# Weight combinations of a seven-product scheme: from sums on VectorE and GpSimd to accumulating DMA transfers

## The chip, the cores and the metric

One core of a Trainium2 chip runs the kernel. The metric is the device time of one execution in microseconds (us); of several runs the median counts, and lower is better.

## What is computed

The reference is one inference step of a decoder layer for 520 tokens (512 of a prompt and 8 single samples): an RMS norm, an input projection, two groups of heads, an output projection, and then a feed-forward part. The change concerns the feed-forward part alone:

```
h = rms_norm(x, g_ffn_pre)
f = (silu(h @ w_gate) * (h @ w_up)) @ w_down
x = x + rms_norm(f, g_ffn_post)
```

h has 2048 features, w_gate and w_up are 2048 x 5632, w_down is 5632 x 2048, all in fp32.

## The kernel before, in words

**Layout.** Activations lie with features on the 128 partitions and 520 tokens in the free dimension, in two halves of 260 tokens (`cols(0)`, `cols(1)`). A product of fp32 values is made of three matmuls on rounded halves: `halved` (L80 to L85) takes a raw weight tile of 128 x 1024 and writes `wh`, a copy rounded by ScalarE (L82), and `wl`, the rest, by VectorE (L84). `split` does the same for activations. Each of the two tags `wh` and `wl` has 4 buffers, so the weights of a product can be prepared at most four products ahead of TensorE.

**The stage of the seven products.** Four of the 44 row blocks of w_gate and w_up are computed plainly. The other 40 go two at a time, so there are 20 passes of the loop over i, each with one call of `seven` for w_gate and one for w_up: 40 calls, here called groups. In a group a 2 x 2 block of weight tiles (rows i and i+1, input halves 0 and 1: w11, w12, w21, w22) meets a 2 x 2 block of activations (feature halves by token halves). Seven products take the place of eight. Each is a call of `term` (L731): 8 blocks of 128 features by 3 matmuls, 24 matmuls of 128 x 260. The activation combinations T1 to T4 are made once, by `combine` (L656), while the last plain blocks run.

**The weights of a group.** `quarters` (L700) gives seven functions, one for each product, which `pieces` calls in order, two products ahead of the one being computed. They load the four raw tiles by SP's DMA queue (L707) and make the combinations: VectorE forms w21 + w22 (L717) and from it s2 = w21 + w22 - w11 (L719); GpSimd forms w11 - w21 (L720) and w12 - s2 (L725). Raw tiles lie in two pools of tag `wr`: `wx` with 4 buffers and `wp` with 3; the sums lie in buffers of `wh` and `wl`. The results in PSUM are joined by VectorE and ScalarE (L750 to L776), and each pass stores its two row blocks to DRAM (fd, L795).

**What sets the order.** A scheduler writes one order of instructions for each engine and each DMA queue when the kernel is built. At run time every engine and queue takes its instructions strictly in that order, and each waits for the semaphores of what it needs. A DMA issued by SP goes by SP's queue, one issued by GpSimd by GpSimd's.

## Time and profile before

| what | value |
| --- | --- |
| median of 3 runs | 2328.52 us (2328.05 to 2331.99) |
| the profiled execution's own time | 2318.88 us |
| its span in the profile | 2317.2 us |
| TensorE (PE) busy | 2266.3 us, 98% of the span |
| VectorE (DVE) busy | 1664.3 us, 72% |
| ScalarE (ACT) busy | 1065.9 us, 46% |
| GpSimd (POOL) busy | 220.6 us, 10% |
| DMA | 310.16 MB, mean 134 GB/s |

The profile is that of one execution; times in it count from the start of its span. PE is the matmul unit, PEld its weight loads. The slices of the page divide the span into 40 equal parts, with one digit of busy tenths for each; PEclk is the granted clock of TensorE. A matmul's end in the profile is modelled, so busy PE is a share of time with matmuls under way, and its count in a stretch tells how many were done.

### The profile page before, as it was taken

The numbers are of one execution on the slowest core, as the hardware profiler recorded it, in microseconds if no ns is written. First come the engines' busy times: TensorE is split into PE (matmuls) and PEld (weight loads), VectorE is DVE, ScalarE is ACT, GpSimd is POOL, SyncE is SP. The second block draws the span as 40 slices with busy tenths as digits, with TensorE's granted clock in tenths as the row PEclk, the third lists the DMA queues.
The fourth block names the chain that finished last, engine by engine and source line by source line (L and its number), as shares of the span: only waits on it lengthen the run. The fifth ranks groups of instructions, "written<-read, shape, count | busy, mean of one in ns | idle before, by whom it ended". The sixth has DMA issues, their size and how long they took to land.

```text
span 2317.2 us, 44793 instructions
## 1 busy us (share of the span) xinstructions
PE 2266.3 (98%) x18548; PEld 2256.2 (97%) x18548; DVE 1664.3 (72%) x2688; ACT 1065.9 (46%) x1607; POOL 220.6 (10%) x116
## 2 busy tenths in 40 slices
PE   8999999999999998999999999999999999999998
PEld 8999999999999998999999999999999999999998
DVE  8398777777555778888888888888888534434367
ACT  7286566666345555444343443444334512212155
POOL 0000000000000000322222222222221000000000
PEclk9999999999999999999999999999999999999999
DMA  6224333443335766543333333333333723332275
GB/s 224 92 88 125 113 114 111 120 120 120 115 110 182 214 209 194 176 158 115 115 110 126 119 115 124 119 120 110 118 119 102 229 92 129 112 113 95 90 240 156
DMA packets 130267, 310.16 MB, mean 134 GB/s; under 512 B 14928, under 2 KB 57360, under 8 KB 130064
## 3 DMA queue, kind: packets, MB, share of 16 engines
q1 hardware_dynamic: 130064, 307.30, 42.7%
q8 instruction: 145, 2.38, 0.4%
q14 instruction: 58, 0.48, 0.1%
HBM read 281.64 MB, written 25.61 MB: 133 GB/s over the span
## 4 chain that ended last, share of the span: by engine, by line
PE 80%; DVE 9%; DMA 8%; ACT 1%; issue 1%; SPq 0%; DVEq 0%; POOL 0%; ACTq 0%; POOLq 0%
PE mm L105 14%; PE mm L104 14%; PE mm L103 14%; PE mm L738 8%; PE mm L736 8%; PE mm L737 8%; DMA bc<-scr 5%; PE ax L738 3%; PE ax L736 3%; PE ax L737 3%; DVE wl L84 2%; PE ax L411 1%; DMA scr<-rows 1%; DMA wr<-w_up 1%; DVE S L483 1%
## 5 line engine op out<-in xcount | busy, mean ns | idle before, releaser
L105 PE MATMUL mm<-A,wl 128*128 128x260 f32 x3616 | 1026.2, 284 | 8.7 <-DVE wl L84 8.4
L103 PE MATMUL mm<-A,wh 128*128 128x260 f32 x3616 | 1031.3, 285 | 2.0 <-ACT wh L82 2.0
L104 PE MATMUL mm<-A,wh 128*128 128x260 f32 x3616 | 1026.0, 284 | 0.0
L82 ACT CAST wh<-wr 128x1024 fp32r<-128x1024 f32 (+1 forms) x460 | 475.4, 1035 | 771.6 <-PE mm L104 475.4
L84 DVE TENSOR_TENSOR wl<-wr,wh 128x1024 fp32r<-128x1024 f32 (+1 forms) x460 | 554.7, 1207 | 268.4 <-ACT wh L82 255.8
L105 PEld LDWEIGHTS mm<-A,wl 128*128 128x128 f32 x3616 | 685.0, 189 | 10.5 <-DVE wl L84 10.3
L103 PEld LDWEIGHTS mm<-A,wh 128*128 128x128 f32 x3616 | 684.8, 189 | 2.5 <-ACT wh L82 2.2
L104 PEld LDWEIGHTS mm<-A,wh 128*128 128x128 f32 x3616 | 685.0, 189 | 0.3
L738 PE MATMUL mm<-A,wl 128*128 128x260 f32 x960 | 271.1, 282 | 0.5 <-DVE wl L84 0.5
L737 PE MATMUL mm<-A,wh 128*128 128x260 f32 x960 | 270.8, 282 | 0.0
L736 PE MATMUL mm<-A,wh 128*128 128x260 f32 x960 | 270.4, 282 | 0.0
L82 ACT CAST wh<-ws 128x1024 fp32r<-128x1024 f32 x120 | 123.8, 1047 | 265.8 <-DVE ws L719 265.8
L811 DVE TENSOR_TENSOR Y<-mm,Y 128x260 f32<-128x260 f32 x160 | 68.4, 427 | 193.0 <-PE mm L105 192.8
L84 DVE TENSOR_TENSOR wl<-ws,wh 128x1024 fp32r<-128x1024 f32 x120 | 188.4, 1570 | 11.8 <-ACT wh L82 10.8
L736 PE MATMUL mm<-T,wh 128*128 128x260 f32 x640 | 181.4, 283 | 1.3 <-ACT wh L82 1.3
L738 PE MATMUL mm<-T,wl 128*128 128x260 f32 x640 | 180.8, 282 | 0.8 <-DVE wl L84 0.8
L738 PEld LDWEIGHTS mm<-A,wl 128*128 128x128 f32 x960 | 180.2, 188 | 0.7 <-DVE wl L84 0.7
L737 PEld LDWEIGHTS mm<-A,wh 128*128 128x128 f32 x960 | 180.8, 188 | 0.0
L736 PEld LDWEIGHTS mm<-A,wh 128*128 128x128 f32 x960 | 180.7, 188 | 0.0
L737 PE MATMUL mm<-T,wh 128*128 128x260 f32 x640 | 180.1, 281 | 0.0
L720 POOL TENSOR_TENSOR wr<-wr 128x1024 f32<-128x1024 f32 x40 | 95.8, 2396 | 478.5 <-DVE ws L717 478.5
L719 DVE TENSOR_TENSOR ws<-ws,wr 128x1024 f32<-128x1024 f32 x40 | 134.3, 3358 | 0.0
(229 smaller groups left out, 3123.2 us busy)
## 6 DMA issues: line engine op xcount, KB each, us to landing
wr<-w_gate SPq DMA_DIRECT2D x96, 512.0 KB, 4.0
wr<-w_up SPq DMA_DIRECT2D x96, 512.0 KB, 4.1
wr<-w_down SPq DMA_DIRECT2D x96, 512.0 KB, 3.6
wr<-w_in SPq DMA_DIRECT2D x92, 512.0 KB, 4.1
wr<-w_out SPq DMA_DIRECT2D x64, 512.0 KB, 3.8
bc<-scr SPq DMA_DIRECT2D x32, 384.0 KB, 5.3
G<-fd SPq DMA_DIRECT2D x44, 260.0 KB, 3.9
fd<-G SPq DMA_DIRECT2D x40, 260.0 KB, 3.6
```

What stands on the lines that cost most here:

```text
L82: act.copy(hi[:, :n], raw[:, :n])
L84: vec.tensor_tensor(out=lo[:, :n], in0=raw[:, :n], in1=hi[:, :n].bitcast(F32), op=ALU.subtract)
L103: pe.matmul(ps[:, :HT], lhsT=wh[:, c], rhs=xh, start=(k == 0), stop=False)
L104: pe.matmul(ps[:, :HT], lhsT=wh[:, c], rhs=xl, start=False, stop=False)
L105: pe.matmul(ps[:, :HT], lhsT=wl[:, c], rhs=xh, start=False, stop=(k == n - 1))
L411: pe.matmul(pl[:, c * 192:(c + 1) * 192], lhsT=kk[:, cg * P:(cg + 1) * P], rhs=qq[:, cg], start=True, stop=True)
L719: vec.tensor_tensor(out=s2, in0=s1, in1=raws["11"], op=ALU.subtract)
L720: nc.gpsimd.tensor_tensor(out=raws["21"], in0=raws["11"], in1=raws["21"], op=ALU.subtract)
L736: pe.matmul(ps, lhsT=wh[:, c], rhs=xh, start=(start and k == 0), stop=False, skip_group_check=not start)
L737: pe.matmul(ps, lhsT=wh[:, c], rhs=xl, start=False, stop=False, skip_group_check=not start)
L738: pe.matmul(ps, lhsT=wl[:, c], rhs=xh, start=False, stop=(k == len(xs) - 1), skip_group_check=not start)
L811: vec.tensor_tensor(out=Y[m][:, cols(h)], in0=ps, in1=Y[m][:, cols(h)], op=ALU.add)
```

## The change

The seven products now come from another set of combinations, in which every weight combination is a plain sum: w21 + w22, then w11 + w21 + w22, then all four, in one tile t[0]; and w11 + w21 in a second tile t[1]. SP loads the first summand of a tile, and GpSimd issues DMA transfers with `accum_op=ALU.add`, which add a weight tile from DRAM to the tile in SBUF. Each next addition to a tile comes after the halving of the value before. The signs move to the activation combinations and to the joins in PSUM; the order of the products changes, the third and the fourth T product use one PSUM bank (`pe_`), and in `combine` two of the four operations of each k go from GpSimd to VectorE. The scratch that the kernel reserves for GpSimd's DMA descriptors goes from 2048 to 4096 bytes. Below, w11 is w[i, 0], w12 is w[i, 1], w21 is w[i + 1, 0] and w22 is w[i + 1, 1]; n1, n5, n2, n6, n3, n4 and n7 are the seven products in their new order (n3, n4 and n7 are the three lambdas).

```diff
--- before.py
+++ after.py
@@ -657,12 +657,12 @@
         c0, c1 = cols(0), cols(1)
         for k in range(8):
             lo, hi = M[k], M[k + 8]
-            vec.tensor_tensor(out=lo[:, c0], in0=lo[:, c1], in1=lo[:, c0], op=ALU.subtract)
+            vec.tensor_tensor(out=lo[:, c0], in0=lo[:, c0], in1=lo[:, c1], op=ALU.subtract)
             T1[k] = split(lo[:, c0], tp, "T", 48)
-            nc.gpsimd.tensor_tensor(out=lo[:, c1], in0=hi[:, c1], in1=lo[:, c1], op=ALU.subtract)
-            vec.tensor_tensor(out=hi[:, c1], in0=hi[:, c1], in1=lo[:, c0], op=ALU.subtract)
+            vec.tensor_tensor(out=lo[:, c1], in0=hi[:, c1], in1=lo[:, c1], op=ALU.subtract)
+            vec.tensor_tensor(out=hi[:, c1], in0=hi[:, c1], in1=lo[:, c0], op=ALU.add)
             T2[k] = split(hi[:, c1], tp, "T", 48)
-            nc.gpsimd.tensor_tensor(out=hi[:, c0], in0=hi[:, c1], in1=hi[:, c0], op=ALU.subtract)
+            vec.tensor_tensor(out=hi[:, c0], in0=hi[:, c1], in1=hi[:, c0], op=ALU.subtract)
             T3[k] = split(lo[:, c1], tp, "T", 48)
             yield
 
@@ -699,34 +699,42 @@
 
     def quarters(w, i, first):
 
-        raws = {}
+
+        t = {}
 
         def load(q, src, pool, bufs):
             pool, bufs = (wp, 3) if first else (pool, bufs)
-            raws[q] = pool.tile([P, 1024], F32, tag="wr", name="wr", bufs=bufs)
-            sp.dma_start(raws[q], src)
-
-        def m1():
-            load("11", w[i, 0], wx, 4)
-            load("21", w[i + 1, 0], wx, 4)
-            load("22", w[i + 1, 1], wp, 3)
-            return halved(raws["11"], 1024)
-
-        def m6():
-            s1 = raws["s1"] = wp.tile([P, 1024], F32, tag="wh", name="ws", bufs=4)
-            vec.tensor_tensor(out=s1, in0=raws["21"], in1=raws["22"], op=ALU.add)
-            s2 = raws["s2"] = wp.tile([P, 1024], F32, tag="wl", name="ws", bufs=4)
-            vec.tensor_tensor(out=s2, in0=s1, in1=raws["11"], op=ALU.subtract)
-            nc.gpsimd.tensor_tensor(out=raws["21"], in0=raws["11"], in1=raws["21"], op=ALU.subtract)
-            load("12", w[i, 1], wp, 3)
-            return halved(s2, 1024)
-
-        def m5():
-            nc.gpsimd.tensor_tensor(out=raws["s2"], in0=raws["12"], in1=raws["s2"], op=ALU.subtract)
-            return halved(raws["s1"], 1024)
-
-        return [m1, m6, m5, lambda: halved(raws["12"], 1024), lambda: halved(raws["21"], 1024),
-                lambda: halved(raws["s2"], 1024), lambda: halved(raws["22"], 1024)]
+            t[q] = pool.tile([P, 1024], F32, tag="wr", name="wr", bufs=bufs)
+            sp.dma_start(t[q], src)
+
+        def add(q, src):
+            nc.gpsimd.dma_start(t[q], src, accum_op=ALU.add)
+
+        def n1():
+            load(1, w[i, 0], wx, 4)
+            load(0, w[i + 1, 0], wx, 4)
+            add(0, w[i + 1, 1])
+            load(2, w[i, 1], wp, 3)
+            o = halved(t[1])
+            add(1, w[i + 1, 0])
+            return o
+
+        def n5():
+            o = halved(t[0])
+            add(0, w[i, 0])
+            return o
+
+        def n2():
+            o = halved(t[2])
+            load(3, w[i + 1, 1], wp, 3)
+            return o
+
+        def n6():
+            o = halved(t[0])
+            add(0, w[i, 1])
+            return o
+
+        return [n1, n5, n2, n6, lambda: halved(t[1]), lambda: halved(t[3]), lambda: halved(t[0])]
 
     def term(ps, xs, start):
 
@@ -744,12 +752,11 @@
 
     def seven(gate):
 
+
         m, u, y1, y2 = (full(gp_, "G", 8) for _ in range(4))
         pa, pb, pc = bank_m(), bank_m(), bank_m()
         term(pa, B11, True)
         act.copy(m[:, c0], pa)
-        term(pb, T2, True)
-        vec.tensor_tensor(out=u[:, c0], in0=pb, in1=m[:, c0], op=ALU.add)
         term(pc, T1, True)
         act.copy(m[:, c1], pc)
         term(pa, B21, False)
@@ -757,23 +764,24 @@
             act.activation(y1[:, c0], pa, AF.Silu)
         else:
             vec.tensor_tensor(out=y1[:, c0], in0=pa, in1=gate[0][:, c0], op=ALU.mult)
+        term(pb, T2, True)
+        vec.tensor_tensor(out=u[:, c0], in0=pb, in1=m[:, c0], op=ALU.subtract)
         pe_ = bank()[:, :HT]
         term(pe_, T3, True)
-        vec.tensor_tensor(out=u[:, c1], in0=pe_, in1=u[:, c0], op=ALU.add)
+        vec.tensor_tensor(out=u[:, c1], in0=u[:, c0], in1=pe_, op=ALU.subtract)
+        vec.tensor_tensor(out=y2[:, c1], in0=u[:, c1], in1=m[:, c1], op=ALU.subtract)
+        term(pe_, T4, False)
+        vec.tensor_tensor(out=y2[:, c0], in0=u[:, c0], in1=pe_, op=ALU.subtract)
+        if gate is None:
+            act.activation(y2, y2, AF.Silu)
+        else:
+            vec.tensor_tensor(out=y2, in0=y2, in1=gate[1], op=ALU.mult)
         term(pc, B22, False)
-        vec.tensor_tensor(out=y1[:, c1], in0=pc, in1=u[:, c0], op=ALU.add)
-        vec.tensor_tensor(out=y2[:, c1], in0=u[:, c1], in1=m[:, c1], op=ALU.add)
-        pd = bank()[:, :HT]
+        vec.tensor_tensor(out=y1[:, c1], in0=pc, in1=u[:, c0], op=ALU.subtract)
         if gate is None:
             act.activation(y1[:, c1], y1[:, c1], AF.Silu)
         else:
             vec.tensor_tensor(out=y1[:, c1], in0=y1[:, c1], in1=gate[0][:, c1], op=ALU.mult)
-        term(pd, T4, True)
-        vec.tensor_tensor(out=y2[:, c0], in0=u[:, c1], in1=pd, op=ALU.subtract)
-        if gate is None:
-            act.activation(y2, y2, AF.Silu)
-        else:
-            vec.tensor_tensor(out=y2, in0=y2, in1=gate[1], op=ALU.mult)
         return y1, y2
 
     for i in range(NSK, FT, 2):
@@ -947,7 +955,7 @@
     import concourse.bacc as bacc
     from concourse.bass_utils import run_bass_kernel_spmd
 
-    nc = bacc.Bacc("TRN2", target_bir_lowering=False, num_devices=1, dynamic_dma_scratch_size=2048)
+    nc = bacc.Bacc("TRN2", target_bir_lowering=False, num_devices=1, dynamic_dma_scratch_size=4096)
     arrays = layouts(**{n: np.asarray(v) for n, v in inputs.items()})
     aps = {n: nc.dram_tensor(n, v.shape, mybir.dt.from_np(v.dtype), kind="ExternalInput").ap() for n, v in arrays.items()}
     for n, s in OUTS.items():
```

**GpSimd's queue, in the stage of the seven products.** The rows are of the third and fourth calls of `seven`: before, the two sums of each group, alternating (a wr or ws tile each).

```order
L720 TENSOR_TENSOR wr_12194<-wr_12192,wr_12194 128x1024 [waits DMAHW0_49,DMAHW7_49,DVE_49,Pool_49]
L725 TENSOR_TENSOR ws_12232<-wr_12235,ws_12232 128x1024 [waits DMAHW2_49,DVE_49]
L720 TENSOR_TENSOR wr_12423<-wr_12421,wr_12423 128x1024 [waits DMAHW3_49,DMAHW4_49,DVE_49,Pool_49]
L725 TENSOR_TENSOR ws_12461<-wr_12464,ws_12461 128x1024 [waits DMAHW7_49,DVE_49]
L720 TENSOR_TENSOR wr_12654<-wr_12652,wr_12654 128x1024 [waits DMAHW0_49,DMAHW6_49,DVE_49,Pool_49]
L725 TENSOR_TENSOR ws_12692<-wr_12695,ws_12692 128x1024 [waits DMAHW5_49,DVE_49]
```

After the change (wr_12419 is t[0] of the third group, wr_12647 t[0] and wr_12645 t[1] of the fourth, wr_12873 t[0] and wr_12871 t[1] of the fifth):

```order
L711 DMA wr_12647<-w_up 128x1024 [waits DMAHW1_49,DMASW0_49]
L711 DMA wr_12419<-w_gate 128x1024 [waits DMASW6_49,DMASW3_49,DVE_49]
L711 DMA wr_12419<-w_gate 128x1024 [waits DMASW3_49,DVE_49]
L711 DMA wr_12645<-w_up 128x1024 [waits DMAHW7_49,DMASW5_49,DVE_49]
L711 DMA wr_12873<-w_gate 128x1024 [waits DMAHW7_49,DMASW4_49]
L711 DMA wr_12647<-w_up 128x1024 [waits DMASW2_49,DVE_49]
L711 DMA wr_12647<-w_up 128x1024 [waits DMASW7_49,DVE_49]
L711 DMA wr_12871<-w_gate 128x1024 [waits DMAHW5_49,DMASW1_49,DVE_49]
```

Sums became transfers, four for each group, and in the queue the first addition to the next group's t[0] (wr_12873) stands ahead of the second and third additions to the present group's t[0] (wr_12647).

**SP's queue, same place.** Before, the loads of the fourth and fifth groups and the stores of the first pass:

```order
L707 DMA wr_12654<-w_up 128x1024 [waits DMAHW0_49,DVE_49]
L707 DMA wr_12656<-w_up 128x1024 [waits DMAHW1_49,DVE_49]
L707 DMA wr_12881<-w_gate 128x1024 [waits DVE_49,DMAHW3_49,Activation_49,Pool_49]
L795 DMA fd_8285<-G_12269 128x520 [waits DVE_49]
L795 DMA fd_8285<-G_12270 128x520 [waits DMAHW4_49,DVE_49]
L707 DMA wr_12695<-w_up 128x1024 [waits DMAHW5_49,DMAHW7_49,DVE_49,Pool_49]
L707 DMA wr_12883<-w_gate 128x1024 [waits DMAHW6_49,DVE_49]
L707 DMA wr_12885<-w_gate 128x1024 [waits DVE_49]
L707 DMA wr_13112<-w_up 128x1024 [waits DVE_49,DMAHW0_49,Activation_49,Pool_49]
```

After the change, the loads of the fourth group (t[1], the tile for n2, t[0], the tile for n4) and the first three of the fifth (t[1], the tile for n2, t[0]):

```order
L708 DMA wr_12645<-w_up 128x1024 [waits DMAHW7_49,DMASW5_49,DVE_49]
L708 DMA wr_12650<-w_up 128x1024 [waits DMAHW2_49,DMAHW0_49,DVE_49]
L708 DMA wr_12647<-w_up 128x1024 [waits DMASW0_49,DVE_49]
L803 DMA fd_8285<-G_12263 128x520 [waits DVE_49]
L708 DMA wr_12725<-w_up 128x1024 [waits DMAHW5_49,DMAHW3_49,DVE_49]
L803 DMA fd_8285<-G_12262 128x520 [waits DMAHW4_49,DVE_49]
L708 DMA wr_12871<-w_gate 128x1024 [waits DMASW1_49,DVE_49]
L708 DMA wr_12876<-w_gate 128x1024 [waits DMAHW6_49,DVE_49]
L708 DMA wr_12873<-w_gate 128x1024 [waits DMAHW7_49,DMASW4_49,DVE_49]
```

The load of t[0] (wr_12873, last row) now waits for the last addition to the tile that lay in its buffer two groups earlier (a semaphore of GpSimd's DMA, DMASW4) and for VectorE, which reads that sum for its last halving.

**TensorE, at the fourth T product.** Before, the last matmuls on B22 (tile mm) and then the fourth T product in a bank of its own (ax_13608):

```order
L737 MATMUL mm_13424<-A_11219,wh_13513 128x260
L738 MATMUL mm_13424<-A_11218,wl_13515 128x260
L736 MATMUL mm_13424<-A_11223,wh_13513 128x260
L737 MATMUL mm_13424<-A_11224,wh_13513 128x260
L738 MATMUL mm_13424<-A_11223,wl_13515 128x260
L736 MATMUL ax_13608<-A_11977,wh_13543 128x260
L737 MATMUL ax_13608<-A_11978,wh_13543 128x260
L738 MATMUL ax_13608<-A_11977,wl_13545 128x260 [waits DVE_49]
L736 MATMUL ax_13608<-A_11981,wh_13543 128x260
```

After the change, the end of n3 (ax_12386), and n4 in the same bank:

```order
L744 MATMUL ax_12386<-T_11969,wh_12328 128x260
L745 MATMUL ax_12386<-T_11970,wh_12328 128x260
L746 MATMUL ax_12386<-T_11969,wl_12330 128x260
L744 MATMUL mm_12266<-A_11127,wh_12387 128x260 [waits Activation_49]
L745 MATMUL mm_12266<-A_11128,wh_12387 128x260
L746 MATMUL mm_12266<-A_11127,wl_12389 128x260 [waits DVE_49]
L744 MATMUL mm_12266<-A_11132,wh_12387 128x260
L745 MATMUL mm_12266<-A_11133,wh_12387 128x260
L744 MATMUL ax_12386<-A_11977,wh_12357 128x260 [waits DVE_49]
```

Five matmuls of n7 (mm_12266) stand between n3 and n4, and the first matmul of n4 waits for VectorE.

## Rows read from the trace of the kernel before

**Rows 1.** The page, part 1 and slices of part 2
```profile
PE 2266.3 (98%) x18548; PEld 2256.2 (97%) x18548; DVE 1664.3 (72%) x2688; ACT 1065.9 (46%) x1607; POOL 220.6 (10%) x116
...
PEclk9999999999999999999999999999999999999999
```

**Rows 2.** Windows: stretch: length, busy (count) of PE, PEld, DVE, ACT, POOL, clock, DMA, GB/s
```profile
975.00:1000.00 25.00, 22.46 (x183) 21.84 (x182) 20.64 (x22) 11.85 (x20) 5.79 (x2) 1.00 0.51 166
1000.00:1100.00 100.00, 100.00 (x834) 100.00 (x834) 86.09 (x77) 41.19 (x53) 24.01 (x10) 1.00 0.39 126
...
1600.00:1700.00 100.00, 100.00 (x834) 100.00 (x833) 85.63 (x77) 41.01 (x55) 24.01 (x10) 1.00 0.37 117
```

**Rows 3.** Instructions of line 717: count, first and last start
```profile
L717 DVE TENSOR_TENSOR ws<-wr x40: 1225/1226/1227, 980.3 to 1767.2; 128x1024 f32<-128x1024 f32 x40
```

**Rows 4.** Groups of instructions by line and shape, 1000 to 1760 us
```profile
L84 DVE TENSOR_TENSOR wl<-wr,wh 128x1024 fp32r<-128x1024 f32 x149 | 182.2, 1223 | 69.3 <-ACT wh L82 58.5 <-DMA wr<-w_up 4.8 <-DMA wr<-w_gate 1.4
...
L82 ACT CAST wh<-wr 128x1024 fp32r<-128x1024 f32 x150 | 157.7, 1051 | 197.1 <-DVE wl L84 135.1 <-PE mm L737 62.0
L719 DVE TENSOR_TENSOR ws<-ws,wr 128x1024 f32<-128x1024 f32 x38 | 127.6, 3357 | 0.0
...
L725 POOL TENSOR_TENSOR ws<-wr,ws 128x1024 f32<-128x1024 f32 x38 | 91.4, 2405 | 136.1 <-DVE wl L84 136.1
L720 POOL TENSOR_TENSOR wr<-wr 128x1024 f32<-128x1024 f32 x38 | 91.0, 2395 | 445.9 <-DVE ws L717 445.9
...
L717 DVE TENSOR_TENSOR ws<-wr 128x1024 f32<-128x1024 f32 x38 | 46.6, 1226 | 21.4 <-PE ax L737 21.4
```

**Rows 5.** Loads of line 707: time from issue to landing, all 160
```profile
L707 SPq DMA_DIRECT2D wr<-w_gate x80: 327/328/423, 971.0 to 1740.1; - x80
...
DMA to landing us min/median/max: 3.2/4.1/7.0
```

**Rows 6.** DMA queues and issues, 1000 to 1760 us
```profile
q1 hardware_dynamic: 27147, 89.01, 37.0%
...
wr<-w_up SPq DMA_DIRECT2D x75, 512.0 KB, 4.2
wr<-w_gate SPq DMA_DIRECT2D x73, 512.0 KB, 4.0
fd<-G SPq DMA_DIRECT2D x38, 260.0 KB, 3.6
```

**Rows 7.** Timelines of DVE, SP and POOL around 1207 to 1215 us: start, length
```profile
1207.87 1.22 DVE L84 TENSOR_TENSOR wl<-ws,wh 128x1024 fp32r<-128x1024 f32 x1 [0.51 <-ACT wh L82]
...
1213.78 1.23 DVE L84 TENSOR_TENSOR wl<-wr,wh 128x1024 fp32r<-128x1024 f32 x1 [1.12 <-ACT wh L82]
...
1215.07 0.33 SPq L707 DMA_DIRECT2D wr<-w_gate  x1
...
1209.17 2.41 POOL L725 TENSOR_TENSOR ws<-wr,ws 128x1024 f32<-128x1024 f32 x1 [3.58 <-DVE wl L84]
```

**Rows 8.** What PE waited for, 975 to 1000 us
```profile
PE mm L736 <- ACT wh L82: 1.3, 1, 1.3
PE mm L738 <- DVE wl L84: 1.2, 2, 0.8
```

**Rows 9.** Timelines of PE and SP at the first group
```profile
970.95 2.56 SPq L707 DMA_DIRECT2D wr<-w_gate  x2
...
984.86 0.28 PE L738 MATMUL mm<-A,wl 128*128 128x260 f32 x1
986.43 0.39 PE L736 MATMUL mm<-T,wh 128*128 128x260 f32 x1 [1.29 <-ACT wh L82]
987.69 0.40 PE L738 MATMUL mm<-T,wl 128*128 128x260 f32 x1 [0.75 <-DVE wl L84]
```

**Rows 10.** While `combine` runs: window, and DVE and POOL groups, 930 to 965 us
```profile
930.00:965.00 35.00, 34.76 (x281) 34.34 (x281) 33.01 (x51) 18.81 (x35) 19.55 (x16) 0.98 0.61 187
...
L663 DVE TENSOR_TENSOR C<-C 128x260 f32<-128x260 f32 x8 | 4.4, 551 | 2.0 <-POOL C L662 2.0
...
L665 POOL TENSOR_TENSOR C<-C 128x260 f32<-128x260 f32 x8 | 12.2, 1527 | 7.5 <-DVE C L663 7.5
```

## The prediction

> **What bounds the kernel now.** I read the page first: TensorE is busy 98% of the span and its granted clock stands at 9 in every slice, that is at the upper of its two levels, 2.4 GHz [rows 1]. Next the windows of the stage that the change touches. From 1000 us on TensorE is busy 100.00 of every 100 us, at full clock, with 834 matmuls in each, while VectorE is busy 86, ScalarE 41 and GpSimd 24 [rows 2]. L717 runs once in each group and gives the beat: 40 of them between 980.3 and 1767.2 us, so (1767.2 - 980.3) / 39 = 20.18 us a group [rows 3]; 168 matmuls at 834 per 100 us make 20.14. So TensorE alone sets the pace, and whatever runs on VectorE and GpSimd lies beside it. The reader should take from this that unloading those two can't shorten a group. The waits of TensorE at the stage's start come to 2.5 us [rows 8], and that is all that the stage could still give.
>
> **What is removed.** VectorE loses 40 pairs of 1.23 and 3.36 us, GpSimd 40 pairs of 2.40 and 2.41 us [rows 4]. Worth on the path: nothing, since TensorE covers it. The collisions between the two engines (L719 takes 3.36 us where L717, alone, takes 1.23) go as well, and are worth nothing for the same reason. In `combine` 16 operations go from GpSimd (1.53 us each on L665) to VectorE, which does the like in 0.55 beside GpSimd and will be a little faster without it; TensorE is idle 0.24 us in those 35 us [rows 10], so I set this at 0. If VectorE fell behind there, the same 0.24 us would grow by a few us at most.
>
> **What is added.** 160 adding transfers of 512 KB, four for each group, issued by GpSimd in queue order. The four plain loads stay. What matters is a chain that goes round once per group. The order of the queues shows it: (1) VectorE ends the last halving of t[0] of group g-1; (2) SP may then load t[0] of group g+1 into that buffer; (3) GpSimd issues the first addition to it; (4) only behind that, in the same queue, stands the second addition to t[0] of group g; (5) n6's weight is halved from it; (6) the third addition; (7) n7's weight of group g is halved, which is step 1 for the next group.
>
> The prices:
> - Hand-over to SP 0.06 us (VectorE's L84 ends at 1215.01, SP issues at 1215.07), to GpSimd 0.08 (1209.09 to 1209.17) [rows 7].
> - The load 4.1 us to landing, the median of 160, with 3.2 and 7.0 as ends [rows 5].
> - A halving 2.31 us: a cast of 1.05, 0.04 between, a subtraction of 1.22 [rows 4, 7].
> - The adding transfer, A, twice, and q, by which the first addition to the next tile holds up the second to this one.
>
> Sum: 0.06 + 4.1 + q + A + 2.31 + 0.08 + A + 2.31 = 8.86 + q + 2A. TensorE covers 20.18, so the chain stays hidden while q + 2A is under 11.3 us.
>
> No row shows an adding transfer, so I bound it. 89.01 MB took 37.0% of 760 us of all 16 engines, which is 3.16 us per MB and 1.66 us for one tile [rows 6]. **Low end:** it lands like a plain load, A = 4.1, and q is one issue, 0.33 us [rows 5]; q + 2A = 8.5, hidden. **High end:** two further passages of a tile through the engines, A = 4.1 + 3.3 = 7.4, and q = 0.33 + 3.3; the chain is 27.3 us, 7.1 too long. **I take** one further passage, because an addition must fetch the tile's old value as well as the weight: A = 5.8, and q = 0.33 + 1.66 = 2.0, since the two transfers share the engines. The chain is then 22.4 us, 2.2 us more than TensorE needs, 39 times: 85 us. The engines themselves speak for this end rather than the low one: per group they carry four loads (6.6 us) and a 260 KB store (0.8 us), and four additions at 3.3 us add 13.3, together 20.8 of 22.4 us, where transfers must wait for one another.
>
> The low end takes an addition for a load. The Trainium skill, in Collectives: The Full Stack, "The bandwidth ceiling", says otherwise of a reducing transfer: the addition itself costs nothing, but it needs two source reads, and these halve the rate. No run here shows that yet; by the row alone the sum would be 0, by the rule the 85 us.
>
> **The first group.** Its load of t[0] is the second of a pair issued from 970.95 to 973.51 [rows 9], so it lands near 977.3; the first addition lands at 983.1, n5 is halved by 985.4, when TensorE has just ended n1 (984.86 and the matmul's 0.28 us). The next two additions, each with a halving, end at 993.6 and about 1002. TensorE, with 24 matmuls or 2.9 us to a product, wants n6 after n5 and n2, near 991.3, and n7 about 3 us earlier than it comes. Stalls of about 0.3 + 2.3 + 3.1 = 5.7 us take the place of the present 2.5 [rows 8]: 3 us more. If A were a load's, this would be about 0.
>
> **One bank for n3 and n4.** n4's first matmul waits until VectorE has read n3's result, 0.42 us; the five matmuls of n7 put between cover 0.6 us at 0.12 each. Set at 0; at most 0.1 us per group, which a stalled TensorE hides.
>
> **Sum:** 85 + 3 = 88 us. The profiled execution (2318.88 us, 1.7 us outside its span) would take 2407; the median of the runs shown is 9.6 us higher, so I predict 2328.5 + 88 = 2417 us.
>
> **Rivals.**
> - *The additions hide.* With q + 2A under 11.3, for instance A = 4.6, nothing in the stage waits, and only the first group's 0 to 3 us remain: about 2331 us. For it speaks that 63% of the engines' time is free now [rows 6]; against it that two additions follow one another inside the chain.
> - *The DMA engines become the bound.* They pass the high end's chain when an addition takes more than (27.3 - 7.5) / 4 = 5 us of all engines, three passages. At five passages, 8.3 us, a group takes 7.5 + 33 = 40.7 us, and the time is 2328.5 + 39 x 20.5 = 3130 us. Nothing in the rows speaks for it, but nothing excludes it.
> - *GpSimd's issue waits for VectorE.* If GpSimd can't do its part of a transfer while VectorE runs, each addition may wait one subtraction, 1.22 us: A = 7.0, q = 3.2, a chain of 26.0 us and 39 x 5.8 + 3 = 230 us: 2559. The 3.36 us of L719 beside GpSimd's L720 show that the two engines hold each other up [rows 4]. The skill's SBUF page, SBUF — State Buffer, "Who interferes with whom", has VectorE's two-input operations collide with GpSimd instructions that read SBUF, not with those that only write. By that this rival falls away.
> - *Faster.* The stalls at the stage's start end, as L719 (3.36 us in the chain before n5) is gone and the first addition comes early: at most 2.5 us [rows 8], 2326. To pass 0.2% it would also need some us from `combine`.
>
> **How the numbers follow.** About 0.2% (4.7 us) is what a measurement of this kernel can tell from no change. Forecast, a chain too long: 0.50, from 2335 to 2615. GpSimd waiting for VectorE: 0.10. DMA engines as the bound: 0.15. Hidden additions: 0.19, of which 0.15 within 0.2% and 0.04 slower. Faster: 0.06. So slower has 0.50 + 0.10 + 0.15 + 0.04 = 0.79, same 0.15, faster 0.06. The range goes from 2328, which takes in the hidden case, to 2615, the high end (39 x 7.1 + 3, and some more in the first group); outside lie the DMA-bound case and most of the faster one, 0.2.
>
> **What would show it.** Right: in the stage TensorE waits for ScalarE's and VectorE's halvings (wh, wl), these for adding transfers; groups of about 22.4 us; adding transfers landing after 5 to 7 us; the load of t[0] leaving just after n7's subtraction; VectorE near 60% busy. Wrong: TensorE still at 100.00 of 100 us (additions hidden), DMA busy near 1.0 throughout (engines as the bound), or a wait of TensorE for VectorE's reads of PSUM.

## The result, and the profile after

The changed kernel takes 2536.25 us (median of 3 runs, 2526.99 to 2536.83), against 2328.52 before: a ratio of 1.0875, 95% interval 1.0834 to 1.0916. The forecast was 2417, with 2328 to 2615 as the range: the direction and the place were right, the loss is 208 us and not 88.

The profiled execution took 2526.99 us, with a span of 2525.3, which is 208.1 more than before. From the first to the last matmul of the stage it has 1006.6 us where the kernel before has 810.9: 195.7 of the 208.1. Another 7.4 lie ahead of the stage (5.2 of them before the 6000th matmul, where nothing was changed and the executions of the kernels here differ by up to 10 us; the cause of the other 2.2 stays open) and 5.1 behind it, where TensorE's waits for the splits of the first stored rows show 2.5.

The page, part 1 and a line of part 2 [rows 1]:

```profile
PE 2335.0 (92%) x18548; PEld 2308.0 (91%) x18548; DVE 1414.1 (56%) x2624; ACT 1066.7 (42%) x1607; POOL 147.2 (6%) x180
...
PEclk9999999999999999999999999998999999999999
```

Every engine is busy for a smaller share of the span than before: the time went into waiting. Windows of the stage [rows 2]:

```profile
1000.00:1100.00 100.00, 87.31 (x676) 85.49 (x675) 44.67 (x55) 32.70 (x43) 14.22 (x17) 0.96 0.79 196
...
1600.00:1700.00 100.00, 86.21 (x660) 84.82 (x659) 44.50 (x54) 32.69 (x42) 13.92 (x16) 0.93 0.72 173
```

660 to 676 matmuls per 100 us where there were 834, and the DMA engines busy 0.72 to 0.79, not near 1.0. The beat, from ScalarE's copy of n1's result, which runs once in a group [rows 3]:

```profile
L759 ACT COPY G<-mm x40: 363/366/368, 999.0 to 1980.9; 128x260 f32<-128x260 f32 x40
```

(1980.9 - 999.0) / 39 = 25.18 us a group, 5.0 above the 20.18 before; times 39 that is 195 us. The additions (L711), and the queues from 1100 to 1900 us [rows 5, 6]:

```profile
L711 POOL DMA_DIRECT2D wr<-w_up x80: 862/862/1150, 1001.2 to 1981.4; - x80
...
DMA to landing us min/median/max: 5.2/6.1/11.0
```

```profile
q0 software_dynamic: 18170, 66.17, 47.9%
q1 hardware_dynamic: 22608, 74.58, 25.2%
```

47.9% of 800 us for 66.17 MB is 5.79 us per MB, 3.04 us of all engines for a 512 KB tile; the loads take 1.42. One turn of the chain in the timelines of SP, POOL, ACT and DVE [rows 7]:

```profile
1488.27 0.33 SPq L708 DMA_DIRECT2D wr<-w_up  x1
...
1505.86 7.97 SPq L708 DMA_DIRECT2D wr<-w_gate  x3
...
1490.07 0.86 POOL L711 DMA_DIRECT2D wr<-w_gate  x1 [9.00 <-DVE wl L84]
1492.25 0.86 POOL L711 DMA_DIRECT2D wr<-w_up  x1 [1.32 <-DMA wr<-w_up]
1492.97 1.04 POOL L711 DMA_DIRECT2D wr<-w_gate  x1
1504.99 0.86 POOL L711 DMA_DIRECT2D wr<-w_gate  x1 [10.98 <-DVE wl L84]
...
1502.39 1.99 ACT L82 CAST wh<-wr 128x1024 fp32r<-128x1024 f32 x2 [7.31 <-DMA wr<-w_gate]
1504.29 0.37 ACT L759 COPY G<-mm 128x260 f32<-128x260 f32 x1
...
1511.16 1.05 ACT L82 CAST wh<-wr 128x1024 fp32r<-128x1024 f32 x1 [5.28 <-DMA wr<-w_gate]
...
1512.24 1.23 DVE L84 TENSOR_TENSOR wl<-wr,wh 128x1024 fp32r<-128x1024 f32 x1 [5.28 <-ACT wh L82]
```

The reader can follow it step by step. SP loads t[0] of the next group (w_up) at 1488.27; GpSimd, which waited for that load, issues its first addition at 1492.25 and, right behind it, this group's second one (w_gate) at 1492.97. ScalarE casts n6's weight when that has landed, at 1502.39. The third addition goes at 1504.99, n7's cast follows at 1511.16, n7's subtraction ends at 1513.47, and the third load in SP's row of three starts just then: the next turn.

What TensorE sees of it, in its waits from 1100 to 1900 us:

```profile
PE mm L744 <- ACT G L759: 90.3, 31, 5.7
...
PE ax L744 <- DVE G L771: 11.6, 11, 1.2
```

The largest wait names ScalarE's copy of a result out of PSUM (L759), which has nothing to do with weights. TensorE's n2 wants that bank. In ScalarE's queue the copy stands behind n6's cast (1502.39, then 1504.29), and the cast waits for the second addition. This is how a late transfer looks two engines on.

The medians over 34 groups beside the forecast:

| step | forecast, us | measured, us |
| --- | --- | --- |
| n7's subtraction to SP's issue | 0.06 | 0.03 |
| load of t[0] | 4.1 | 3.63 |
| landing to the first addition's issue | 0 | 0.53 |
| first addition's issue to the second's landing (q + A) | 7.8 | 0.64 + 8.88 |
| landing to cast, twice | 0 | 0.20 |
| two halvings | 4.62 | 4.61 |
| subtraction to the third addition's issue | 0.08 | 0.29 |
| third addition (A) | 5.8 | 6.01 |
| sum | 22.4 | 24.8 |

The mean is 25.2, since single additions land up to 2 us later than the median.

The DMA packets in the trace, the pieces of 4 KB in which the engines move a transfer, show how the second addition comes to its 8.88 us (medians of 32 groups). The third addition, which has nothing under way ahead of it in GpSimd's queue, sends its first packet 1.58 us after its issue. The second sends its first after 4.57 us, just as the last packets of the first addition start: the two don't share the engines, they pass one after the other, and the first lands after 6.1 us, hardly later than the third. The first addition's first packet is itself 0.9 us late (2.51 us), because the addition to this group's t[1], issued 2.3 us ahead of it (1490.07 in the timeline), is still passing. The forecast's sum doesn't have that one.

### The profile page after: what moved, and what is told of

Its sections match the earlier page's. It is cut to its first block, busy times and chain, and to the rows that moved or that the text cites. A ratio compares the mean times of both kernels' runs of the same rounds, so it can differ in the third digit from the quotient of the medians.

```text
span 2525.3 us, 44887 instructions
## 1 busy us (share of the span) xinstructions
PE 2335.0 (92%) x18548; PEld 2308.0 (91%) x18548; DVE 1414.1 (56%) x2624; ACT 1066.7 (42%) x1607; POOL 147.2 (6%) x180
## 4 chain that ended last, share of the span: by engine, by line
PE 52%; DMA 30%; DVE 8%; issue 5%; ACT 3%; POOL 1%; ACTq 0%; POOLq 0%; SPq 0%; DVEq 0%
PE mm L105 13%; PE mm L104 13%; PE mm L103 13%; DMA wr<-w_gate 12%; DMA wr<-w_up 11%; DMA bc<-scr 5%; PE mm L744 2%; PE mm L745 2%; PE mm L746 2%; ACT wh L82 2%; DVE wl L84 2%; PE ax L411 1%; PE ax L744 1%; POOL wr L711 1%; PE ax L745 1%
## 5 line engine op out<-in xcount | busy, mean ns | idle before, releaser
L82 ACT CAST wh<-wr 128x1024 fp32r<-128x1024 f32 (+1 forms) x580 | 596.9, 1035 | 1235.2 <-PE mm L104 480.8
L84 DVE TENSOR_TENSOR wl<-wr,wh 128x1024 fp32r<-128x1024 f32 (+1 forms) x580 | 696.8, 1208 | 633.6 <-ACT wh L82 618.5
L103 PE MATMUL mm<-A,wh 128*128 128x260 f32 x3616 | 1032.3, 286 | 4.9 <-ACT wh L82 3.3
L105 PE MATMUL mm<-A,wl 128*128 128x260 f32 x3616 | 1027.2, 284 | 9.8 <-DVE wl L84 9.8
L104 PE MATMUL mm<-A,wh 128*128 128x260 f32 x3616 | 1026.6, 284 | 1.1 <-DVE A L113 1.0
L105 PEld LDWEIGHTS mm<-A,wl 128*128 128x128 f32 x3616 | 685.3, 190 | 11.1 <-DVE wl L84 10.9
L103 PEld LDWEIGHTS mm<-A,wh 128*128 128x128 f32 x3616 | 685.3, 190 | 6.2 <-ACT wh L82 3.8
L104 PEld LDWEIGHTS mm<-A,wh 128*128 128x128 f32 x3616 | 686.3, 190 | 1.8 <-DVE A L113 1.5
L744 PE MATMUL mm<-A,wh 128*128 128x260 f32 x960 | 294.9, 307 | 115.2 <-ACT G L759 114.6
L744 PEld LDWEIGHTS mm<-A,wh 128*128 128x128 f32 x960 | 199.6, 208 | 123.9 <-ACT G L759 122.9
L746 PE MATMUL mm<-A,wl 128*128 128x260 f32 x960 | 290.1, 302 | 3.1 <-DVE wl L84 3.0
L745 PE MATMUL mm<-A,wh 128*128 128x260 f32 x960 | 290.0, 302 | 0.0
L746 PEld LDWEIGHTS mm<-A,wl 128*128 128x128 f32 x960 | 200.5, 209 | 4.5 <-DVE wl L84 4.3
L745 PEld LDWEIGHTS mm<-A,wh 128*128 128x128 f32 x960 | 200.4, 209 | 0.0
L711 POOL DMA_DIRECT2D wr<-w_gate x80 | 73.3, 916 | 843.7 <-DMA fd<-t 420.5
L744 PEld LDWEIGHTS mm<-T,wh 128*128 128x128 f32 x640 | 122.3, 191 | 0.0
L745 PEld LDWEIGHTS mm<-T,wh 128*128 128x128 f32 x640 | 121.8, 190 | 0.0
L746 PEld LDWEIGHTS mm<-T,wl 128*128 128x128 f32 x640 | 121.5, 190 | 0.0
```

The lines of the kernel that those rows point to most:

```text
L82: act.copy(hi[:, :n], raw[:, :n])
L84: vec.tensor_tensor(out=lo[:, :n], in0=raw[:, :n], in1=hi[:, :n].bitcast(F32), op=ALU.subtract)
L103: pe.matmul(ps[:, :HT], lhsT=wh[:, c], rhs=xh, start=(k == 0), stop=False)
L104: pe.matmul(ps[:, :HT], lhsT=wh[:, c], rhs=xl, start=False, stop=False)
L105: pe.matmul(ps[:, :HT], lhsT=wl[:, c], rhs=xh, start=False, stop=(k == n - 1))
L711: nc.gpsimd.dma_start(t[q], src, accum_op=ALU.add)
```

## The experiments

Theory: the chain as forecast sets the beat, and its place is made by the order in GpSimd's queue. Rivals: the DMA engines' load as the bound; the price of an addition or of GpSimd's issue as such, wherever it stands; the shared bank and `combine`. Times are medians, beside the kernel before on the same chip (2321 to 2325 us). The changed kernel, run again, took 2525.13 us, ratio 1.0862 (1.0846 to 1.0879).

### What an addition costs

**e3_plain_writes**

```diff
-            nc.gpsimd.dma_start(t[q], src, accum_op=ALU.add)
+            nc.gpsimd.dma_start(t[q], src)
```

> The four additions of a group are plain transfers by GpSimd to the same tiles, in the same order with the same waits: what is left out is the addition itself, so the tiles hold the last weight only. Chain theory with a price by the engines (an adding tile takes 3.04 us of all 16 engines, a plain one 1.42): the second addition falls from 8.9 to about 5.5 us, the third from 6.0 to about 4.5, the chain from 25.2 to 20 to 21 us: 2335 to 2375 us. If the price is GpSimd's way of issuing (descriptors, its port, VectorE in the way), each stays within 0.5 us of what it was: 2500 us or more.

2329.04 us, ratio 1.0021 (1.0011 to 1.0032), 6 us below the expected range. The lines of L711, a window, and the queues from 1100 to 1800 us:

```profile
L711 POOL DMA_DIRECT2D wr<-w_up x80: 527/527/544, 1000.4 to 1790.0; - x80
...
DMA to landing us min/median/max: 3.4/4.2/8.0
```

```profile
1300.00:1400.00 100.00, 100.00 (x828) 99.41 (x827) 56.57 (x67) 41.84 (x52) 10.55 (x20) 1.00 0.67 220
```

```profile
q1 hardware_dynamic: 24336, 79.06, 34.4%
q0 software_dynamic: 19584, 71.31, 31.7%
```

The same number of transfers, from the same queue, with the same waits, hides but for 0.2%. A plain one lands after 4.2 us, like a load, and takes 31.7% of 700 us for 136 tiles, 1.63 us each. So the price is the addition, 3.04 / 1.63 = 1.9 times the engines' time. The packets agree: a tile is 128 packets of 4 KB in both kernels, and the median one takes 328 ns in an addition and 159 in a plain transfer. The second addition's place fell from 8.9 to 5.0 us, the third's from 6.0 to 3.9. Of these last 2.1 us GpSimd's issue makes 0.33 (862 against 527 ns), so GpSimd's way of issuing is a small part, and VectorE runs beside it here too.

**e4_half_columns**

```diff
+            nc.gpsimd.dma_start(t[q][:, 0:512], src[:, 0:512], accum_op=ALU.add)
```

> Each addition covers 512 of the 1024 columns; what is left out is the sum in the other half. Same number of descriptors of half the length. Chain theory with a price by bytes: the second addition falls by half of both passages (3.04 us) and the third by half of one (1.5 us), the chain from 25.2 to about 20.7 us: 2345 to 2400 us. If most of the price is fixed for each transfer or each descriptor, 2480 us or more.

2333.20 us, ratio 1.0033 (1.0020 to 1.0046), 12 us below the expected range. The second addition took 5.3 us, the third 4.1. The queue:

```profile
q0 software_dynamic: 19440, 35.40, 33.4%
```

33.4% of 700 us for 135 half tiles is 1.73 us each, 0.57 of a whole tile's 3.04: most of the price goes with the bytes.

**e11_first_half**: the same edit on the first addition alone.

> Only the first addition of each group, which stands ahead of the second in GpSimd's queue, covers 512 of the 1024 columns; what is left out is that sum in the other half. The second and third additions are whole and keep their places. If the first addition holds up the second by its own passage through the engines (3.04 us for a whole tile), the second lands 1.5 us sooner after its issue (7.4 in place of 8.9) and the chain of 25.2 us becomes 23.7: about 2477 us, 2460 to 2490. If it holds it up only by the issue on GpSimd (0.64 us), nothing changes: 2536 us within 10.

2500.13 us, ratio 1.0748 (1.0719 to 1.0778), and 25 us below the changed kernel on the same chip, 24.7 us a group: between the two expectations, and a miss by its numbers. The first addition landed 1.5 us sooner (4.6 for 6.1), the second only 0.45 (8.43 for 8.88). The packets show both halves of it (medians of 32 groups). The second addition's first packet leaves 1.3 us sooner, 3.26 us after its issue in place of 4.57, as the passage of the first one would have it. But its own packets then take 4.73 us from first to last in place of 3.80, and more of SP's traffic passes meanwhile, 0.52 MB in place of 0.43. How much of these 0.9 us is due to that stays open.

### Where the chain lies

**e8_swap_two**: the first addition for the next group is issued in n5, right behind this group's second one, and GpSimd keeps the program's order.

```diff
+            tc.keep_in_program_order(nc.gpsimd.dma_start(t[q], src, accum_op=ALU.add))
...
         def n5():
             o = halved(t[0])
             add(0, w[i, 0])
+            if me + 1 < len(ahead):
+                ahead[me + 1]()
```

(`ahead[k]` loads t[0] of group k and adds w22 to it, so that load moves in the program too. The additions are pinned as in e1 below, where the order alone is kept.)

> Changed from the kernel after in one place of GpSimd's queue: the first addition to the next group's t[0] goes out right behind the second addition to this group's, where it had stood right ahead of it. Bytes, buffers and additions are the same. Chain theory: the load and the first addition no longer precede the second addition, which runs alone (6.0 to 6.4 us where it took 8.9 behind the other); what is left of a cycle goes through ScalarE's order (n7's cast, n1's, n5's): second addition 6.2, halving 2.4, 0.3, third addition 6.0 to 7.5, casts of n7, n1 and n5 3.3, subtraction 1.2, 0.3, together 19.7 to 21.2 us a group against TensorE's 20.2: 2330 to 2375 us. DMA engines as the bound: no change from 2536 us. Price of an addition in itself as the cause, wherever it stands: above 2450 us.

2389.67 us, ratio 1.0295 (1.0276 to 1.0313). Two neighbours in one queue change places, and some 135 us of the loss are gone, with the same bytes and more busy engines (0.84). The timeline of GpSimd and the beat:

```profile
1419.39 0.86 POOL L715 DMA_DIRECT2D wr<-w_gate  x1 [1.53 <-DVE wl L84]
1419.92 1.22 POOL L715 DMA_DIRECT2D wr<-w_up  x1
1428.66 0.86 POOL L715 DMA_DIRECT2D wr<-w_gate  x1 [7.51 <-DVE wl L84]
```

```profile
L771 ACT COPY G<-mm x40: 359/366/375, 988.9 to 1837.7; 128x260 f32<-128x260 f32 x40
```

The second addition (w_gate, 1419.39) no longer waits for a load, and lands after 6.3 us (median); the first (w_up) now takes 9.0, and nobody waits for it. The beat of 21.8 us is above the 19.7 to 21.2 expected, and the time above its 2375; what is left is taken up below. The engines' load as the bound falls, and so does the price of an addition wherever it stands.

**e1_program_order**: the pinned additions alone, without the move: the first addition for the next group then stands behind the third.

> The four additions of a group leave GpSimd in the order in which the program names them, so the first addition to the next group's t[0] stands behind the third to this group's, not ahead of the second. Chain theory (one chain per group: n7's halving, load of t[0], first addition, second addition behind it, n6's halving, third addition, n7's halving; 25.2 us): the load leaves the chain, since the tile's buffer was freed a group ago. What is left of a cycle runs in GpSimd's queue: third addition, 0.6 us, first addition of the next group beside it 8.8, halving 2.4, 0.3, second addition 6.0 (8.8 if t[1]'s is under way), halving 2.4, 0.3, together 20.8 to 23.6 us a group, so 2350 to 2470 us. DMA engines as the bound: the same bytes, so no change from 2536 us. GpSimd's issue held up by VectorE: the same issues, so a chain shorter by the load alone (4 us), but each addition still 2.7 us or more above a load's 3.6 even where it runs alone.

2426.96 us, ratio 1.0447 (1.0425 to 1.0468), 23.0 us a group, both within the expectation. The load is out of the chain, but the first addition, issued 0.5 us behind the third, lands after 10.4 us and n5 waits for it.

**e2_six_buffers**

```diff
-            load(0, w[i + 1, 0], wx, 4)
+            load(0, w[i + 1, 0], wx, 6)
```

(and the pool's `bufs`, and the load of t[1], alike)

> The pool of t[0] and t[1] has 6 buffers in place of 4, so a tile of the next group but one may be loaded a group earlier; with it GpSimd's queue also comes out in the program's order. Chain theory: the load is out of the chain in either case, and the cycle in GpSimd's queue is the one of the run in program order, so the time is within 20 us of that run's (2350 to 2470 us). If the wait for a free buffer is what counts and not the queue's order, this run is faster than that one by 40 us or more. DMA engines as the bound: 2536 us.

2534.26 us, ratio 1.0899 (1.0882 to 1.0915): no gain at all, and the expectation fails at its first step. It assumed that GpSimd's queue would come out in the program's order, and it did not. The kernel as built has there (wr_12193, wr_12419, wr_12647, wr_12873: t[0] of the second to the fifth group):

```
L711 DMA wr_12647<-w_up 128x1024 [waits DMAHW7_49]
L711 DMA wr_12193<-w_up 128x1024 [waits DMASW7_49,DMASW1_49,DVE_49]
L711 DMA wr_12417<-w_gate 128x1024 [waits DMAHW3_49,DVE_49]
L711 DMA wr_12873<-w_gate 128x1024 [waits DMAHW3_49,DMASW3_49,DMASW1_49]
L711 DMA wr_12419<-w_gate 128x1024 [waits DMASW6_49,DVE_49]
```

With a buffer pair more, the scheduler simply takes the first addition one group further ahead: that of the fifth group (wr_12873) stands before the second one of the third (wr_12419). Its load still starts when n7 has been halved, of the group three before, so the chain is the same, 25.5 us. More buffers don't help where the queue is filled up to the buffers again.

### VectorE for the first sum

**e7_first_sum_vector**: no first addition; VectorE adds w22, which n4 needs anyway.

```diff
         def n5():
+            if not first:
+                vec.tensor_tensor(out=t[0], in0=t[0], in1=t[3], op=ALU.add)
+                load(2, w[i, 1], wp, 3)
             o = halved(t[0])
             add(0, w[i, 0])
```

> The first of the three sums in t[0], w21 + w22, is made by VectorE from the two raw tiles that are loaded anyway (1.2 us), except in the first group; three additions a group by transfers remain. Chain theory: as in the run with the two swapped, the load and the first addition leave the chain, and a quarter of the adding traffic goes: 19.5 to 20.5 us a group, 2328 to 2350 us. If additions as such are too slow, or the bound lies elsewhere in the stage, 2450 us or more.

2475.17 us, ratio 1.0661 (1.0645 to 1.0678), 24.1 us a group: a miss. VectorE's timeline:

```profile
1437.61 1.23 DVE L727 TENSOR_TENSOR wr<-wr 128x1024 f32<-128x1024 f32 x1 [2.36 <-DMA wr<-w_gate]
1438.75 0.42 DVE L778 TENSOR_TENSOR G<-G,ax 128x260 f32<-128x260 f32 x1
1439.09 1.22 DVE L84 TENSOR_TENSOR wl<-wr,wh 128x1024 fp32r<-128x1024 f32 x1
```

and its order as built, around that place in another group (wr_16051: t[0] of one group, wr_16279: of the next):

```
L727 TENSOR_TENSOR wr_16279<-wr_16279,wr_16281 128x1024 [waits DMAHW1_49,DMAHW0_49,DVE_49]
L778 TENSOR_TENSOR G_15895<-G_15895,ax_16018 128x260 [waits DVE_49,PE_49]
L84 TENSOR_TENSOR wl_16091<-wr_16051,wh_16089 128x1024 [waits Activation_49]
```

The next group's sum, which waits 2.36 us for its load, stands ahead of this group's n5. This looks like the same trap on another engine: the load after n7, something of the next group behind it, this group's second addition behind that.

**e7b_sum_in_order**: that sum kept in the program's order on VectorE.

> The run with w21 + w22 on VectorE, with that sum kept in the program's order on VectorE: it then stands behind n7's subtraction of the group before, where the scheduler had put the next group's sum, which waits for its load, ahead of this group's n5. If that place made the 24 us a group of that run, they fall to 20.2 to 21.8 us: 2330 to 2395 us. If the sum itself or the buffers of the raw tiles made it, the time stays at 2475 us within 15.

2613.21 us, ratio 1.1244 (1.1223 to 1.1264), 27.3 us a group: slower still. In the program's order the sum stands behind all joins of the group before, which wait for TensorE's n4; the second addition comes after that, and TensorE's n6 after the second addition, so by this order the chain goes round through TensorE. ScalarE's waits from 1100 to 1700 us fit it:

```profile
ACT wh L82 <- DVE wr L727: 101.6, 22, 9.0
```

That the place of the sum matters is shown, since nothing else was edited; the price that I gave for the new place was wrong. That its place in e7 made that run's 24.1 us is argued from the order and the waits, and no run shows it by a gain.

### What else the change holds

**e5_combine_back** (the two lines of `combine` as before) and **e6_own_bank** (`pd = bank()[:, :HT]` for n4 again):

> In combine the two sums of each k that went from GpSimd to VectorE are back on GpSimd; all else as in the kernel after. Of the 208 us the stage's groups hold 195; if combine holds part of the other 13, this run is 4 to 10 us faster than 2536 us; if not, within 3 us of it.

2523.62 us, ratio 1.0867 (1.0841 to 1.0893). It is 12 us below the 2536, but beside the kernel before on the same chip the ratio is about that of the changed kernel run again, 1.0862. From the 6000th matmul to the stage the changed kernel takes 210.7 us, this one 210.9, the kernel before 208.6: `combine` is not the cause of what is lost there.

> n4 gets a PSUM bank of its own again in place of n3's; all else as in the kernel after. Chain theory: TensorE's 13.9 us of waits for VectorE's reads of that bank in the stage go, but the chain of transfers sets the pace, so the time stays within 6 us of 2536 us. If the shared bank costs time, 10 us or more are gained.

2533.24 us, ratio 1.0911 (1.0880 to 1.0942): no gain, while the chain covers it.

### What is left when the chain is short

After the swap 21.6 us a group remained in the middle of the stage. **e10_n5_first** puts n5 ahead of n1 in the list of products and in `seven`, on top of the swap.

> The run with the two additions swapped, and with n5 computed ahead of n1, so that ScalarE casts n5's weight right behind n7's of the group before, and the addition to t[1] comes behind the second addition to t[0]. If the remaining 1.4 us a group over TensorE's 20.2 (21.6 measured) come from the cycle through ScalarE's and VectorE's order, one cast (1.05 us) and some queueing leave it: 20.2 to 20.7 us a group, 2328 to 2350 us. If they come from the engines' load (0.84 busy), no change: 2380 to 2395 us.

2411.12 us, ratio 1.0372 (1.0344 to 1.0400): slower than without it. The second addition now runs alone (5.6 us), but the one to t[1] goes out behind it and the next group's first, lands after 9.0 us, and holds up the third addition (7.4 for 6.0). The wait was moved, so this told nothing of the cause.

**e12_n7_late**, on top of the swap, computes n7 of each group after n1 of the next.

```diff
-            queue.extend(quarters(a[nm], i, i == NSK and nm == "w_gate"))
+            q7 = quarters(a[nm], i, i == NSK and nm == "w_gate")
+            queue.extend(q7[:1] + tail + q7[1:6])
+            tail = q7[6:]
...
         term(pa, B11, True)
         act.copy(m[:, c0], pa)
+        if late:
+            late.pop()()
```

(`late` holds n7's matmuls and joins of the group before.)

> The run with the two additions swapped, and with n7 of each group computed after n1 of the next, so that ScalarE casts n1's weight ahead of n7's, and TensorE asks for n7 2.9 us later. Additions, bytes, buffers and GpSimd's order stay. Cycle through ScalarE's and VectorE's order as what is left: 21.6 us less a cast (1.05) and the gaps at it (0.5), about 20.0, under TensorE's 20.2: 20.2 to 20.7 us a group, 2328 to 2350 us. Load of the DMA engines (0.84 busy in that run) as what is left: 21.4 us or more, 2375 to 2395 us.

2345.92 us, ratio 1.0098 (1.0080 to 1.0116), within the expectation. A window:

```profile
1300.00:1400.00 100.00, 100.00 (x825) 99.35 (x824) 54.59 (x66) 42.11 (x53) 17.09 (x20) 1.00 0.90 216
```

TensorE is at 100 of 100 us again, and the DMA engines at 0.90 carry all of it. So the rest came from the order of the halvings, not from the engines' load. The new order also spreads the additions: the one to t[1] has landed before the second is issued, which takes 5.5 us in place of 6.3.

**e13_late_and_bank** adds a bank of its own for n4.

> The run with n7 late, and n4 in a PSUM bank of its own. In that run TensorE was at 100 of 100 us, yet did 824 matmuls where the kernel before does 834; twice a group, at n4's first two matmuls, the next one came 0.1 us late, 0.19 us a group. If n4's wait for VectorE's read of n3's bank makes these, they go: 20.2 us a group in place of 20.4, 834 matmuls per 100 us, and 8 us off 2346: 2334 to 2341 us. If something else in the stage slows TensorE by 1% (the transfers, at 0.90 of all engines), 824 stay, and 2346 us within 3.

2332.93 us, ratio 1.0041 (1.0028 to 1.0054), 1 us below the expectation. The same window:

```profile
1300.00:1400.00 100.00, 100.00 (x833) 100.00 (x833) 55.65 (x67) 42.09 (x53) 16.75 (x20) 1.00 0.91 219
```

833 matmuls: the shared bank costs 0.2 us a group once nothing covers it. The remaining 10 us are nearly all in the first groups, where TensorE still waits 7.1 us for ScalarE's copy: after the first two groups the stage is 7.9 us behind the kernel before, at its end 9.0. All four additions stay, and the kernel is 0.4% slower than the one before, which no version here beats.

## Why the prediction was right and wrong

- **What bounds before, and the removed sums at 0.** Right: e13 has VectorE at 56 of 100 us where it was at 86 [rows 2], and is no faster.
- **The chain.** Right in each link: n7, load, first addition, second behind it, n6, third, n7. The swap (e8) shows that the place of the first addition makes it.
- **q, the step that failed.** I charged the first addition as holding up the second by an issue and one plain passage, 0.33 + 1.66 = 2.0 us, "since the two transfers share the engines". It holds it up by 3.5: the second lands 9.5 us after the first's issue, where an addition that follows none takes 6.0. The two don't share: the second's first packet waits for the first's last ones, and these take an addition's time, not a plain transfer's. The right figure stood in the same paragraph, in the high end's q and in the 3.3 us of the engines that I gave an addition (3.04 measured). With q = 3.6 the chain would have been 24.0. I also left out the addition to t[1], which goes ahead of both. In e12, where it has landed by then, an addition 0.64 us behind another sends its first packet after 4.13 us in place of 4.57, so it is worth some 0.4 us by my estimate.
- **A.** 5.8 forecast, 6.0 measured for the third addition: right. The Trainium skill, Collectives: The Full Stack, "The bandwidth ceiling", says that a reducing transfer needs two source reads and that these halve the rate. The trace agrees: 3.04 us against 1.63 from the same queue. That the second read is the reason no run here shows.
- **Hand-overs.** 0.14 forecast, 1.05 measured. I took them from rows in which one engine follows another, but from a landing to GpSimd's issue it is 0.53, to a cast 0.10, and from a subtraction to an addition's issue 0.29. The load came 0.5 us sooner than its median before.
- **From chain to time.** Together q +1.5, A +0.4, hand-overs +0.9, load -0.5 and the late tails +0.4 make about 2.8 us, an eighth of the chain. TensorE covers 20.2 of it, so the excess went from 2.2 to 5.0 us, and 85 us became 195. A small error in a sum that is nearly covered is a large one in the loss.
- **First group, bank, combine.** Set at 3, 0 and 0. The stage's 195.7 us leave less than 1 for the first group beside the 39 beats; with the chain hidden (e13) the first two groups lose 7.9, so the 3 was too little there. The bank is right while hidden, and 0.2 us a group, not at most 0.1, when not (e13). `combine` is right (e5).
- **Signs.** The load of t[0] left just after n7's subtraction (0.03 us), and the first and third additions landed within 5 to 7 us, as said. TensorE's wait had another name than said: 90.3 us stand at ScalarE's copy and 2.8 at wh and wl, because the late cast holds up the copy. VectorE was busy 45 of 100 us, not 60, as the groups took longer.
- **Rivals.** Hidden additions: q + 2A had to be under 11.3 and was 15.5. DMA engines as the bound: 0.72 to 0.79 busy, and e13 runs them at 0.91 with 833 matmuls in 100 us. GpSimd's issue waiting for VectorE: its 2559 us came nearer than the forecast, by chance, since A was 6.0 and not 7.0; in e3 plain transfers from GpSimd land after 4.2 us beside the same VectorE work, like the loads before (4.1 [rows 5]). The Trainium skill, SBUF — State Buffer, "Who interferes with whom", has VectorE's operations with two inputs collide with GpSimd instructions that read SBUF, not with those that only write it. e3 fits this, but shows nothing of what GpSimd reads for a transfer.

## What to carry to other kernels

Here a transfer that adds to its target cost 1.9 times the engines' time of a plain one, and a second one queued behind it began only when the first had passed, so charge the first at its own price, not at a load's. When an in-order queue has work of the next round ahead of this round's, look what that work waits for: here two neighbours that changed places were worth 135 us, while more buffers (e2) or another engine for the sum (e7) left a load and work of the next round ahead of this round's. Where a chain is nearly covered, give the range by the chain's error, not by the loss's.

## What the runs showed of the hardware

- An adding transfer of 512 KB took 3.04 us of all 16 engines, a plain one from the same queue 1.63, SP's loads 1.42; half the columns, 1.73. To landing an addition needed 5.5 us alone (e12), 6.3 with another's end before it (e8), 8.9 behind one issued 0.64 us earlier, 10.4 behind one issued 0.5 us earlier (e1). GpSimd's additions pass one after another: the second's first packet starts 5.21 us after the first's issue, the first's last one 5.23 after it (medians). The Trainium skill, DMA: Bandwidth & Descriptors, "SWDGE vs HWDGE vs iDMA", has one queue for all of GpSimd's transfers, which each engine serves in turn with the others. The first half agrees with these packets; of the second, the traces show only that SP's packets pass within an addition (0.43 MB in the second's 3.80 us).
- GpSimd's own part is 862 ns for an addition and 527 for a plain transfer.
- In the stage TensorE's mean granted clock fell to 0.93 to 0.97. From 1100 to 1900 us it is at 0.50 of full (1.2 GHz) for 96 us in 23 stretches, and at 1.00 (2.4 GHz) otherwise. In 22 of the 23 it fell during or right after a wait of TensorE for ScalarE's copy, of 1.8 to 5.7 us, and 47% of the matmuls of n2, which follow that wait, ran at the lower level, against 3% or less of any other product's. There the next matmul came after 215 ns in place of 120. n2 works on A, and so the matmuls on A are the longer ones in the mean:

```profile
L744 PE MATMUL mm<-A,wh 128*128 128x260 f32 x757 | 234.0, 309 | 90.9 <-ACT G L759 90.3 <-ACT wh L82 0.6
...
L744 PE MATMUL mm<-T,wh 128*128 128x260 f32 x504 | 143.8, 285 | 0.0
```

The chain of transfers covers this loss too. e12 and e13, without the waits, are at 1.00 from 1300 to 1400 us.
